# A decoder block on one core: seven products for the first ff2 block as well, and a new order around the output projection

## The chip, the cores and the metric

One core of a Trainium2 chip (trn2) runs one launch of the kernel. The metric is device time in microseconds (us), the median of 3 runs. Lower is better.

## What is computed

A post-norm decoder block on x of shape (1, 256, 2048), all in float32:

```
proj = x @ w_in                       # 2048 x 9216
q, k, v, u, vb, ga, gb = split(proj)
y_a = dilated_attention(q, k, v) @ w_proj_a
y_b = (u * spatial_gate(layer_norm(vb))) @ w_proj_b
mix = (sigmoid(ga) * y_a + sigmoid(gb) * y_b) @ w_out
h   = layer_norm(ALPHA * x + mix, ln1_gain, ln1_bias)
ff  = square(relu(h @ w_ff1 + b_ff1)) @ w_ff2 + b_ff2      # 2048 -> 8192 -> 2048
out = layer_norm(ALPHA * h + ff, ln2_gain, ln2_bias)
```

## The kernel before

**Chunks, pieces, steps.** Weights come from HBM in chunks of 512 rows by 512 columns (1 MB) through SP's DMA queue into three `raw` buffers. Float32 accuracy comes from a split: each number is a high part and a low part, and three matmuls (high by high, high by low, low by high) stand for one product. A chunk is two pieces of two k-tiles (128 rows each). For a piece ACT copies the high part (L188) and DVE subtracts to get the low part (`emit_low`, L157); both lie in one `w2` buffer. A step is one piece's matmuls. The lists `pieces` and `steps` are filled first; the main loop (L979 to 993) then writes, step by step: the splits for which a buffer is free (six ring buffers, so the splits run some five pieces ahead; a group can have spare buffers of its own as `tags`), the high and low parts of activations that wait in `rounds`, one or two finished tiles from `later`, the step's matmuls, and the side work that `at(step, ...)` put there. Each engine works off its own instructions in that order. A new chunk's load is issued when the last piece of a buffer is split.

**Groups.** A group is 512 output columns. With stationary weights (L252 with 512 columns, L254 with 256) run the in-projection, `w_pa`, `w_pb` and ff1; with stationary activations (L240 to 242) the output projection and ff2. When a weight-stationary group ends, ACT copies the half of each of its four banks (L273, with a bias L275), DVE adds (L277), and only then is a bank free.

**Seven products.** For the first two of four column groups, two row halves by two token halves by two column groups make eight block products; the kernel gets them by seven (P1 to P7) of 512 columns, as in Strassen's scheme (`products`, L634; L212 to 214 on PE). P1 uses the weight tile b0 as loaded, P5, P6 and P4 use it after one, two and three more blocks were added onto it, P7 uses b1, the sum of two blocks, and P3 and P2 use chunks. b0 and b1 are loaded and added to by POOL's DMA queue: `held_load` (L620; L623 loads, L625 accumulates onto b1) and `held_add` (L632, accumulates onto b0). The next block can be added onto b0 only when the low part of its last piece is made. The summed activations (`ca`) are made on DVE by `sum_of_acts` (L567, subtractions and additions at L575 to 578, high and low parts at L93 and L94). `collect` (L684) adds the products up at the very end for ff2, and behind P2 for the output projection.

**Order of the program.** In-projection with attention and gMLP between; then four times `w_pa` and `w_pb` (1024 rows, 8 pieces); the output projection's column group 2 in four chunks, with P7, P4, P3 and P2 behind one chunk each; its groups 0 and 1, then 3 (two passes, one for each token half); the first norm (`ln1_part`); ff1 of block 0 in two groups; then for b = 1 to 7 the two ff1 groups of block b and ff2 of block b-1 (1024 rows). Where block b-1 is in `SUMMED` (L608: blocks 1 to 6), its first two column groups are seven products, and `mixed(b)` (L696) lays the pieces of ff1 (F, 8 pieces for each group), of the products (2 each) and of ff2's columns 2 and 3 (E, 4 each) by the list ORDER (L37). I call such a stretch a period. Otherwise both ff1 groups come first, then four plain ff2 groups. P1, P6 and P5 of the output projection stand between `w_pa` and `w_pb`:

```
if i >= 2:
    add_product(("P1", "P6")[i - 2])      # behind w_pa's third and fourth group
...
if i == 2:
    at(len(steps), held_load, uo, 1)      # b1, behind w_pb's third group
    add_product("P5")
```

**The second residual.** The row tensors `y` hold the normalised rows. `residual2` makes for each of 4 column groups one bias part, b_ff2 += ALPHA * ln1_b, and for both token halves y = y * (ALPHA * ln1_g) and then y += that bias (L564, L565). The three vectors are broadcast over 128 partitions (1 MB each, the `wide` tiles) and loaded on SP's queue behind the ff1 chunks of block 1.

Of the kernel before, what the change touches and what calls it, by code (L numbers as in the profile page):

```python
# [26 lines left out]
G = 8  # L27
DB = G * 128
FF = 4 * D
CW = 512  # L30
# [5 lines left out]
NCT = CW // P  # L36
ORDER = ("F F F P1 F P1 F F F P5 F P5 F F F P6 F P6 F P3 P3 F P7 F P7 F "  # L37
         "E P2 E P2 E E P4 E P4 E E E").split()
WARM = (256, 256, 256, 128)
EARLY = 3  # L40
NBUCKET = 32
# [30 lines left out]
def block_kernel(ctx: ExitStack, tc: tile.TileContext, xT, x, w_in, rel_bias, lnv_g, lnv_b, wsT, b_sp,  # L72
# [61 lines left out]
    def add_group(g, sizes=None):  # L134
        hs = add_pieces(g, sizes)
        for h in hs:
            add_step(h, "all", h == hs[0], h == hs[-1])
# [162 lines left out]
    tiles = {}  # L300
# [252 lines left out]
    def load_wide(key, src, tag):  # L553
        tiles[key] = big.tile([P, D], F32, name="wide", tag=tag)
        nc.sync.dma_start(tiles[key], bcast(src, D))

    def residual2(c, part):
        sl = slice(c * CW, (c + 1) * CW)
        bb = tiles["b_ff2"][:, sl]
        if part == 0:  # L560
            nc.vector.scalar_tensor_tensor(bb, tiles["ln1_b"][:, sl], ALPHA, bb, op0=ALU.mult, op1=ALU.add)
        else:
            y = tiles["y", part - 1][:, sl]
            nc.vector.scalar_tensor_tensor(y, y, ALPHA, tiles["ln1_g"][:, sl], op0=ALU.mult, op1=ALU.mult)  # L564
            nc.vector.tensor_tensor(y, y, bb, op=ALU.add)  # L565

    def sum_of_acts(tags, ot, q):  # L567
# [37 lines left out]
        return ev  # L605

    NB = FF // 1024
    SUMMED = range(1, NB - 1)  # L608

    def ff_unit(blk):
        return SimpleNamespace(w=w_ff2, row=blk * 1024, act=lambda r, k: tiles["a", 2 * blk + r][:, k, :],
                               tags=("S10", "S11"), acc="S12", key="ff", scale=None)
# [81 lines left out]
    def mixed(b):  # L696

        made = {"F": [ff1_group(2 * b), ff1_group(2 * b + 1)], "E": [ff2(b - 1, c) for c in (2, 3)]}
        prods = products(ff_unit(b - 1), ff_unit(b) if b in SUMMED else None)
        if b - 1 == SUMMED[0]:  # L700
            for i in range(2):
                at(len(steps) - 7, held_load, ff_unit(b - 1), i)
        left = {}

        queue = {"F": [], "E": []}
        for name in ORDER:
            if name in prods:
                if name not in left:
                    hs = prods[name]()
                    left[name] = [(h, h == hs[0], h == hs[-1]) for h in hs]  # L710
                q = left[name]
            else:
                q = queue[name]
                if not q:
                    g = made[name].pop(0)
                    for c in range(g.nk // KC):
                        q.append((g, c, None))
                if q[0][2] is None:
                    g, c, _ = q.pop(0)
                    hs = add_pieces(g, None, (c,))  # L720
                    q[:0] = [(h, c == 0 and h == hs[0], c == g.nk // KC - 1 and h == hs[-1]) for h in hs]
            h, f, l = q.pop(0)
            add_step(h, "all", f, l)
# [71 lines left out]
    def quad(key):  # L795
        return lambda k: tiles[key][k // 4][:, k % 4, :]
# [5 lines left out]
    def at(s, f, *a):  # L802
        side.setdefault(s, []).append((f, a))
# [35 lines left out]
    def add_product(name):  # L839
        hs = prods[name]()  # L840
        for h in hs:
            add_step(h, "all", h == hs[0], h == hs[-1])

    at(len(steps) + 8, held_load, uo, 0)
    for i in range(4):
        add_group(Group(w_pa, i * CW, 8, quad("attnT"), "ws", ev_ya(i)))
        if i >= 2:
            add_product(("P1", "P6")[i - 2])
        if i == 2:
            for k in range(4):  # L850
                at(len(steps) - 1 + k, lambda k=k: sum_of_acts(("S6", "W"), k, tiles["G", 1][:, 0, k, :]))
        add_group(Group(w_pb, i * CW, 8, quad("gmlpT"), "ws", ev_yb(i), after=start_residual if i == 3 else None))
        if i == 2:
            at(len(steps), held_load, uo, 1)
            add_product("P5")

    g = Group(w_out, 2 * CW, 16, quad("merged"), "as", ev_out(2))
    for c, name in enumerate(("P7", "P4", "P3", "P2")):
# [7 lines left out]
                        ev_out(i, False), row=1024))  # L866


    spare = ("A0", "A1", "A2", "A3", "S6")
    wide = tuple(f"S1{i}" for i in range(4))  # L870
    at(len(steps), free.extend, spare)
    g = Group(w_out, 3 * CW, 16, quad("merged"), "as", ev_out(3), tags=spare)
# [17 lines left out]
        return Group(w_ff1, f * CW, 16, quad("hT"), "ws", ev_ff1(f))  # L890

    def ff1(f):
        add_group(Group(w_ff1, f * CW, 16, quad("hT"), "ws", ev_ff1(f), tags=wide if f == 1 else ()))

    def ff2(blk, c):
        return Group(w_ff2, c * CW, 8, lambda k: tiles["a", 2 * blk + k // NCT][:, k % NCT, :], "as",
                     ev_ff2(blk, c), row=blk * 1024, tags=LATE if blk == NB - 1 else ())

    ff1(1)
    s = len(steps)  # L900
    for i in range(4):
        for j in range(3):
            at(s + 13 + 3 * i + j, residual2, i, j)
    for b in range(1, NB):
        j = len(chunks)
        if b - 1 in SUMMED:
            mixed(b)
            continue
        ff1(2 * b)
        ff1(2 * b + 1)  # L910
        if b == 1:
            for i, a in enumerate((("ln1_b", ln1_b, "S11"), ("b_ff2", b_ff2, "S10"), ("ln1_g", ln1_g, "S12"))):
                load_post[j + 2 * i] = [lambda a=a: load_wide(*a)]
        for c in range(4):
            add_group(ff2(b - 1, c))
    at(len(steps), free.extend, LATE[:4])
# [111 lines left out]
```

## Time and profile before

| | before |
|---|---|
| median of 3 runs | 1326.16 us (1325.57 to 1326.43) |
| profiled execution | 1326.2 us, its span 1324.5 us |
| mean granted clock of TensorE | 0.998 |
| PE busy | 1312.9 us, 99% |
| DVE busy | 939.0 us, 71% |
| ACT busy | 691.0 us, 52% |
| DMA | 288.83 MB, mean 218 GB/s |

The span runs from the first to the last record of the profiled execution; its own time has 1.7 us more around it. PE is TensorE's matmuls, PEld its weight loads (beside them), DVE is VectorE, ACT is ScalarE, POOL is GpSimd (here almost only an issuer of DMAs), SP the engine that issues the other DMAs. A busy share is an average over stages; what bounds a stage is read from its waits. PE is at `w_pa` and `w_pb` until 527.88, then at the output projection until about 607, from 746.23 to 833.90 on the period of b = 2, and each later period takes 86.92.

### The profile page before, as it was taken

What the parts mean: (1) busy time and instruction counts of PE and PEld (TensorE: products, weight loads), DVE (VectorE), ACT (ScalarE), POOL (GpSimd) and SP (SyncE); (2) the same over time, 40 slices, a digit from 0 to 9 for tenths busy, and PEclk for the clock granted to TensorE, in tenths of its full rate; (3) what the DMA queues carried; (4) which work ended last, traced back from release to release, by engine and by line L of the source; (5) the groups of instructions that cost most, each with busy time, mean ns of one, the idle gap of its engine ahead of it and who ended that gap; (6) DMA issues with size and microseconds to landing.
All of it is one profiled execution on the core that took longest, in us unless ns stands there. A gap on an engine that the chain in (4) does not pass through costs nothing. (4 is left out here: it accounts for less than half of the span.)

```text
span 1324.5 us, 17423 instructions
## 1 busy us (share of the span) xinstructions
PE 1312.9 (99%) x6832; PEld 1111.0 (84%) x6832; DVE 939.0 (71%) x1426; ACT 691.0 (52%) x938; POOL 51.7 (4%) x57
## 2 busy tenths in 40 slices
PE   9999999999999999999999999999999999999998
PEld 6888888888888888889888888888888888888886
DVE  6554678565545689788769768678677796786776
ACT  4444465454544556545545366455555564555641
POOL 0000000000000001000000100010000000100000
PEclk9999999999999999999999999999999999999999
DMA  9866545546555569772874988987887879978561
GB/s 321 289 195 206 176 137 182 191 160 222 191 191 190 187 169 291 244 230 71 283 255 148 284 219 289 248 242 247 217 280 229 237 242 251 252 224 236 178 254 64
DMA packets 140003, 288.83 MB, mean 218 GB/s; under 512 B 5256, under 2 KB 7824, under 8 KB 139024
## 3 DMA queue, kind: packets, MB, share of 16 engines
q1 hardware_dynamic: 120592, 240.26, 53.5%
q0 software_dynamic: 19184, 47.20, 16.8%
q8 instruction: 53, 0.87, 0.3%
q10 hardware_dynamic: 144, 0.26, 0.1%
q14 instruction: 30, 0.25, 0.1%
HBM read 285.59 MB, written 2.11 MB: 217 GB/s over the span
## 5 line engine op out<-in xcount | busy, mean ns | idle before, releaser
L157 DVE TENSOR_TENSOR w<-raw,w 128x1024 fp32r<-128x1024 f32 (+1 forms) x438 | 529.2, 1218 | 300.8 <-ACT w L188 299.7
L188 ACT ACTIVATE w<-raw 128x1024 fp32r<-128x1024 f32 (+1 forms) x438 | 456.7, 1053 | 411.8 <-PE mm L254 289.7
L252 PE MATMUL mm<-hT,w 128*128 128x512 f32 x960 | 339.4, 394 | 0.8 <-DVE sum L277 0.8
L252 PE MATMUL mm<-xs,w 128*128 128x512 f32 x896 | 315.7, 395 | 0.0
L254 PE MATMUL mm<-hT,w 128*128 128x256 f32 x1024 | 276.0, 279 | 0.0
L254 PE MATMUL mm<-xs,w 128*128 128x256 f32 x896 | 250.0, 279 | 0.0
L252 PEld LDWEIGHTS mm<-hT,w 128*128 128x128 f32 x960 | 180.0, 187 | 44.3 <-DVE sum L277 1.1
L252 PEld LDWEIGHTS mm<-xs,w 128*128 128x128 f32 x896 | 167.9, 187 | 39.5
L254 PEld LDWEIGHTS mm<-hT,w 128*128 128x128 f32 x1024 | 188.0, 188 | 2.7
L254 PEld LDWEIGHTS mm<-xs,w 128*128 128x128 f32 x896 | 168.0, 187 | 0.2
L242 PE MATMUL mm<-w,a 128*128 128x512 f32 (+1 forms) x328 | 128.1, 390 | 0.0
L241 PE MATMUL mm<-w,a 128*128 128x512 f32 (+1 forms) x328 | 128.0, 390 | 0.0
L240 PE MATMUL mm<-w,a 128*128 128x512 f32 (+1 forms) x328 | 127.8, 390 | 0.0
L157 DVE TENSOR_TENSOR w<-held,w 128x1024 fp32r<-128x1024 f32 x70 | 85.6, 1223 | 39.3 <-ACT w L188 38.9
L188 ACT ACTIVATE w<-held 128x1024 fp32r<-128x1024 f32 x70 | 73.9, 1058 | 64.7 <-PE mm L242 26.6
L240 PEld LDWEIGHTS mm<-w,a 128*128 128x128 f32 x328 | 61.8, 188 | 14.3
L242 PEld LDWEIGHTS mm<-w,a 128*128 128x128 f32 x328 | 61.7, 188 | 14.0
L241 PEld LDWEIGHTS mm<-w,a 128*128 128x128 f32 x328 | 61.8, 188 | 13.9
L240 PE MATMUL mm<-w,xs 128*128 128x512 f32 x120 | 49.4, 412 | 0.3 <-ACT w L188 0.3
L241 PE MATMUL mm<-w,xs 128*128 128x512 f32 x120 | 47.7, 397 | 1.3 <-DVE w L157 1.3
L277 DVE TENSOR_TENSOR sum<-mm,half 128x256 f32<-128x256 f32 x136 | 48.9, 418 | 0.0
L242 PE MATMUL mm<-w,xs 128*128 128x512 f32 x120 | 47.6, 397 | 0.0
(193 smaller groups left out, 1512.8 us busy)
## 6 DMA issues: line engine op xcount, KB each, us to landing
raw<-in_w_ff_dram SPq DMA_DIRECT2D x116, 1024.0 KB, 6.5
raw<-in_w_in_dram SPq DMA_DIRECT2D x68, 1024.0 KB, 5.1
held<-in_w_ff_dram POOLq DMA_DIRECT2D x36, 1024.0 KB, 8.5
raw<-in_w_out_dram SPq DMA_DIRECT2D x14, 1024.0 KB, 5.4
raw<-in_w_pa_dram SPq DMA_DIRECT2D x8, 1024.0 KB, 5.1
raw<-in_w_pb_dram SPq DMA_DIRECT2D x8, 1024.0 KB, 5.1
held<-in_w_out_dram POOLq DMA_DIRECT2D x6, 1024.0 KB, 8.5
raw<-in_w_in_dram SPq DMA_DIRECT2D x6, 512.0 KB, 7.2
```

The source lines that it names most:

```text
L157: nc.vector.tensor_tensor(h["lo"], sl, f32(h["hi"]), op=ALU.subtract)
L188: nc.scalar.activation(h["hi"], source(h), AF.Copy)
L240: nc.tensor.matmul(p, ah, hi[:, kk, cs], start=first and kk == 0, stop=False)
L241: nc.tensor.matmul(p, ah, lo[:, kk, cs], start=False, stop=False)
L242: nc.tensor.matmul(p, al, hi[:, kk, cs], start=False, stop=last and kk == n - 1)
L252: nc.tensor.matmul(p, hi[:, kk, ws_], av, start=st, stop=False)
L254: nc.tensor.matmul(p[:, :S], lo[:, kk, ws_], av[:, :S], start=False, stop=en)
L277: nc.vector.tensor_tensor(s, p[:, :S], t, op=ALU.add)
```

## The change

- **Block 0 has seven products too** (SUMMED from 0). Its period (b = 1) follows a list of its own, FIRST: the products keep their order but P7, which comes behind P2.
- **The rows of the second norm's residual come earlier.** ln1_b and ln1_g are loaded, on SP's queue, into the buffers A2 and A3 ahead of the output projection's last group, which loses these two as spare buffers for its splits; b_ff2 comes near the end of the first ff1 group into S11. The second ff1 group keeps two spare buffers of four.
- **`residual2` is cut in two kinds of parts.** The factors (1, 2) lie beside the second ff1 group; the bias parts (0) and the additions (3, 4) lie in the first period.
- **Output projection.** P5 comes behind `w_pa`'s fourth group and P6 behind `w_pb`'s fourth (before: P5 behind `w_pb`'s third, P6 behind `w_pa`'s fourth). Summed activations are made in every second step. The load of b1 is written three steps ahead of the end of `w_pb`'s fourth group.
- **Held tiles of block 0** are loaded at the second step of the second ff1 group (b0) and at the 14th step of the period (b1).

```diff
 NCT = CW // P
 ORDER = ("F F F P1 F P1 F F F P5 F P5 F F F P6 F P6 F P3 P3 F P7 F P7 F "
          "E P2 E P2 E E P4 E P4 E E E").split()
+FIRST = ("F F F P1 F P1 F F F P5 F P5 F F F P6 F P6 F P3 P3 F "
+         "E P2 E P2 E F P7 E P7 F E P4 E P4 E E").split()
 WARM = (256, 256, 256, 128)
 EARLY = 3
 NBUCKET = 32
...
         bb = tiles["b_ff2"][:, sl]
         if part == 0:
             nc.vector.scalar_tensor_tensor(bb, tiles["ln1_b"][:, sl], ALPHA, bb, op0=ALU.mult, op1=ALU.add)
-        else:
+        elif part < 3:
             y = tiles["y", part - 1][:, sl]
             nc.vector.scalar_tensor_tensor(y, y, ALPHA, tiles["ln1_g"][:, sl], op0=ALU.mult, op1=ALU.mult)
+        else:
+            y = tiles["y", part - 3][:, sl]
             nc.vector.tensor_tensor(y, y, bb, op=ALU.add)
 
     def sum_of_acts(tags, ot, q):
...
         return ev
 
     NB = FF // 1024
-    SUMMED = range(1, NB - 1)
+    SUMMED = range(0, NB - 1)
 
 
 
...
 
         made = {"F": [ff1_group(2 * b), ff1_group(2 * b + 1)], "E": [ff2(b - 1, c) for c in (2, 3)]}
         prods = products(ff_unit(b - 1), ff_unit(b) if b in SUMMED else None)
-        if b - 1 == SUMMED[0]:
-            for i in range(2):
-                at(len(steps) - 7, held_load, ff_unit(b - 1), i)
         left = {}
 
         queue = {"F": [], "E": []}
-        for name in ORDER:
+        for name in FIRST if b == 1 else ORDER:
             if name in prods:
                 if name not in left:
                     hs = prods[name]()
...
     for i in range(4):
         add_group(Group(w_pa, i * CW, 8, quad("attnT"), "ws", ev_ya(i)))
         if i >= 2:
-            add_product(("P1", "P6")[i - 2])
+            add_product(("P1", "P5")[i - 2])
         if i == 2:
             for k in range(4):
-                at(len(steps) - 1 + k, lambda k=k: sum_of_acts(("S6", "W"), k, tiles["G", 1][:, 0, k, :]))
+                at(len(steps) - 1 + 2 * k, lambda k=k: sum_of_acts(("S6", "W"), k, tiles["G", 1][:, 0, k, :]))
         add_group(Group(w_pb, i * CW, 8, quad("gmlpT"), "ws", ev_yb(i), after=start_residual if i == 3 else None))
-        if i == 2:
-            at(len(steps), held_load, uo, 1)
-            add_product("P5")
+        if i == 3:
+            at(len(steps) - 3, held_load, uo, 1)
+            add_product("P6")
 
     g = Group(w_out, 2 * CW, 16, quad("merged"), "as", ev_out(2))
     for c, name in enumerate(("P7", "P4", "P3", "P2")):
...
                         ev_out(i, False), row=1024))
 
 
-    spare = ("A0", "A1", "A2", "A3", "S6")
+    spare = ("A0", "A1", "S6")
+    for i, a in enumerate((("ln1_b", ln1_b, "A2"), ("ln1_g", ln1_g, "A3"))):
+        at(len(steps) - 6 + 3 * i, load_wide, *a)
     wide = tuple(f"S1{i}" for i in range(4))
     at(len(steps), free.extend, spare)
     g = Group(w_out, 3 * CW, 16, quad("merged"), "as", ev_out(3), tags=spare)
...
         return Group(w_ff1, f * CW, 16, quad("hT"), "ws", ev_ff1(f))
 
     def ff1(f):
-        add_group(Group(w_ff1, f * CW, 16, quad("hT"), "ws", ev_ff1(f), tags=wide if f == 1 else ()))
+        add_group(Group(w_ff1, f * CW, 16, quad("hT"), "ws", ev_ff1(f), tags=wide[2:] if f == 1 else ()))
 
     def ff2(blk, c):
         return Group(w_ff2, c * CW, 8, lambda k: tiles["a", 2 * blk + k // NCT][:, k % NCT, :], "as",
                      ev_ff2(blk, c), row=blk * 1024, tags=LATE if blk == NB - 1 else ())
 
+
+    s = len(steps)
+    at(s - 10, load_wide, "b_ff2", b_ff2, "S11")
+    at(s + 1, held_load, ff_unit(0), 0)
     ff1(1)
-    s = len(steps)
+    e = len(steps)
     for i in range(4):
-        for j in range(3):
-            at(s + 13 + 3 * i + j, residual2, i, j)
+        for j in (1, 2):
+            at(s + 4 * (j - 1) + i, residual2, i, j)
+        at(e + i, residual2, i, 0)
+        for j in (3, 4):
+            at(e + 1 + i + 4 * (j - 3), residual2, i, j)
+    at(e + 13, held_load, ff_unit(0), 1)
     for b in range(1, NB):
-        j = len(chunks)
         if b - 1 in SUMMED:
             mixed(b)
             continue
         ff1(2 * b)
         ff1(2 * b + 1)
-        if b == 1:
-            for i, a in enumerate((("ln1_b", ln1_b, "S11"), ("b_ff2", b_ff2, "S10"), ("ln1_g", ln1_g, "S12"))):
-                load_post[j + 2 * i] = [lambda a=a: load_wide(*a)]
         for c in range(4):
             add_group(ff2(b - 1, c))
     at(len(steps), free.extend, LATE[:4])
```

On POOL, around the output projection (held_3848 is b0; held_4339 before and held_4510 after are b1; y are the two loads of x's rows), before:

```order
L623 DMA held_3848<-in_w_out_dram 128x4x512
L632 DMA held_3848<-in_w_out_dram 128x4x512 x2
L623 DMA held_4339<-in_w_out_dram 128x4x512
L625 DMA held_4339<-in_w_out_dram 128x4x512
L632 DMA held_3848<-in_w_out_dram 128x4x512
L499 DMA y_4589<-in_x_dram 128x2048
```

and with the change:

```order
L627 DMA held_3848<-in_w_out_dram 128x4x512
L636 DMA held_3848<-in_w_out_dram 128x4x512 x3
L627 DMA held_4510<-in_w_out_dram 128x4x512
L629 DMA held_4510<-in_w_out_dram 128x4x512
L501 DMA y_4569<-in_x_dram 128x2048
```

The third addition onto b0 stood behind b1's load and accumulation; it now stands ahead of both.

On ACT, around the splits of b1 for P7 (L188 is L190 with the change, the high part of a piece; L273 is L275, the halves of `w_pb`'s fourth group; acc gets P1 or P5), before:

```order
L188 ACTIVATE w2_4489<-raw_4328 128x1024
L188 ACTIVATE w2_4515<-held_4339 128x1024
L188 ACTIVATE w2_4535<-held_4339 128x1024
L188 ACTIVATE w2_4554<-raw_4410 128x1024
L273 ACTIVATE half_4573<-mm_4495 128x256
L273 ACTIVATE half_4577<-mm_4500 128x256
L273 ACTIVATE half_4581<-mm_4505 128x256
L273 ACTIVATE half_4585<-mm_4510 128x256
L188 ACTIVATE w2_4594<-raw_4410 128x1024
```

and with the change:

```order
L190 ACTIVATE w2_4454<-held_3848 128x1024
L665 ACTIVATE acc_4184<-aux_4447 128x512
L190 ACTIVATE w2_4465<-held_3848 128x1024
L190 ACTIVATE w2_4490<-raw_4251 128x1024
L190 ACTIVATE w2_4513<-raw_4251 128x1024
L190 ACTIVATE w2_4534<-held_4510 128x1024
L275 ACTIVATE half_4553<-mm_4470 128x256
L275 ACTIVATE half_4557<-mm_4475 128x256
L275 ACTIVATE half_4561<-mm_4480 128x256
L275 ACTIVATE half_4565<-mm_4485 128x256
L190 ACTIVATE w2_4574<-held_4510 128x1024
```

Both splits of b1 stood ahead of the four halves; now the second stands behind them, and P6's two splits of b0 stand a little ahead of b1's.

On DVE, one round in the new first period, with the change (sq is a squared tile of ff1, cb and ca the summed activations; y and wide belong to the residual; w2 is a piece):

```order
L601 SCALAR_TENSOR_TENSOR sq_5777<-sum_5722 128x256
L579 TENSOR_TENSOR cb_5779<-q0_5487,sq_5777 128x128
L580 TENSOR_TENSOR cb_5779<-q0_5487 128x128
L581 TENSOR_TENSOR cb_5779<-cb_5779,q0_5487 128x128
L582 TENSOR_TENSOR cb_5779<-sq_5777,cb_5779 128x128
L569 TENSOR_TENSOR y_4569<-y_4569,wide_5461 128x512
L563 SCALAR_TENSOR_TENSOR wide_5461<-wide_4887,wide_5461 128x512
L159 TENSOR_TENSOR w2_5802<-raw_5530,w2_5802 128x1024
L96 TENSOR_TENSOR a_5737<-sq_5777,a_5737 128x256
L96 TENSOR_TENSOR ca_5740<-cb_5779,ca_5740 128x2x128
L96 TENSOR_TENSOR ca_5741<-cb_5779,ca_5741 128x2x128
```

In block 0 there were no cb and ca before; the additions of the residual (L569) and its bias parts (L563) stand between them now.

## Rows read from the trace of the kernel before

**Rows 1.** First part of the page: busy us, share of the span, instructions.

```profile
PE 1312.9 (99%) x6832; PEld 1111.0 (84%) x6832; DVE 939.0 (71%) x1426; ACT 691.0 (52%) x938; POOL 51.7 (4%) x57
```

**Rows 2.** Timeline of PE: start us, duration, engine, line, operation, tile, shapes, count.

```profile
701.25 0.40 PE L240 MATMUL mm<-w,a 128*128 128x512 f32 x1
...
746.23 0.40 PE L252 MATMUL mm<-hT,w 128*128 128x512 f32 x1
```

**Rows 3.** Timeline of PE at three waits (in brackets: idle us, releaser).

```profile
501.31 0.40 PE L213 MATMUL aux<-w,ca 128*128 128x512 f32 x1
502.23 0.50 PE L214 MATMUL aux<-w,ca 128*128 128x512 f32 x1 [0.53 <-DVE ca L94]
...
634.15 0.28 PE L254 MATMUL mm<-hT,w 128*128 128x256 f32 x1
635.24 0.51 PE L252 MATMUL mm<-hT,w 128*128 128x512 f32 x1 [0.81 <-DVE sum L277]
...
768.65 0.39 PE L212 MATMUL aux<-w,ca 128*128 128x512 f32 x1
769.51 0.50 PE L213 MATMUL aux<-w,ca 128*128 128x512 f32 x1 [0.48 <-DVE w L157]
```

**Rows 4.** Timeline of ACT: halves and splits, output projection and second ff1 group.

```profile
514.44 0.92 ACT L273 ACTIVATE half<-mm 128x256 f32<-128x256 f32 x3
...
516.50 2.00 ACT L188 ACTIVATE w<-raw 128x1024 fp32r<-128x1024 f32 x2
...
631.40 2.01 ACT L188 ACTIVATE w<-raw 128x1024 fp32r<-128x1024 f32 x2 [6.20 <-DMA raw<-in_w_ff_dram]
```

**Rows 5.** Timeline of PE: first matmuls of w_pa 4, P6, w_pb 4, out 2, P7.

```profile
502.57 0.40 PE L252 MATMUL mm<-attnT,w 128*128 128x512 f32 x1
...
513.77 0.40 PE L212 MATMUL aux<-w,ca 128*128 128x512 f32 x1
...
516.57 0.39 PE L252 MATMUL mm<-gmlpT,w 128*128 128x512 f32 x1
...
527.88 0.40 PE L240 MATMUL mm<-w,merged 128*128 128x512 f32 x1
...
533.50 0.40 PE L212 MATMUL aux<-w,ca 128*128 128x512 f32 x1
```

**Rows 6.** Timeline of DVE: low part of P5's second piece (tile b0).

```profile
508.51 1.22 DVE L157 TENSOR_TENSOR w<-held,w 128x1024 fp32r<-128x1024 f32 x1
```

**Rows 7.** Timeline of POOL: issue of b1's accumulation and of b0's third sum.

```profile
508.07 1.26 POOL L625 DMA_DIRECT2D held<-in_w_out_dram  x1 [6.29 <-DMA held<-in_w_out_dram]
510.02 1.27 POOL L632 DMA_DIRECT2D held<-in_w_out_dram  x1 [0.69 <-DVE w L157]
```

**Rows 8.** Held tiles: issue to landing; whole run, then the two issues of rows 7.

```profile
DMA to landing us min/median/max: 5.5/8.5/18.0
...
DMA to landing us min/median/max: 8.9/11.6/14.2
```

**Rows 9.** POOL's DMA queue: packets, MB, share; 505 to 506 (load), 516 to 517 (accumulation).

```profile
q0 software_dynamic: 94, 0.39, 100.9%
...
q0 software_dynamic: 102, 0.20, 111.6%
```

**Rows 10.** The chain that ended last: start us, us, what.

```profile
749.05 18.01 DMA held<-in_w_ff_dram
```

**Rows 11.** Timeline of DVE: third ff1 group's sums; two rounds' beginnings in the next period.

```profile
700.93 1.45 DVE L277 TENSOR_TENSOR sum<-mm,half 128x256 f32<-128x256 f32 x4
...
708.89 0.42 DVE L597 SCALAR_TENSOR_TENSOR sq<-sum 128x256 f32<-128x256 f32 x1
...
713.75 0.42 DVE L597 SCALAR_TENSOR_TENSOR sq<-sum 128x256 f32<-128x256 f32 x1
```

**Rows 12.** Stretches: us, busy of PE, PEld, DVE, ACT, POOL, granted clock, DMA share, GB/s.

```profile
1313.00:1316.00 3.00, 3.00 (x9) 1.27 (x8) 2.76 (x8) 1.06 (x4) 0.00 (x0) 1.00 0.00 0
1318.50:1324.50 6.00, 1.35 (x2) 0.30 (x2) 1.77 (x4) 0.60 (x1) 0.00 (x0) 0.57 0.49 175
```

## The prediction

> **What bounds the kernel now.** The page's first part comes first: PE is busy for 99% of the span [rows 1]. Less work on another engine can therefore hardly shorten the run; a change counts by the matmuls that it takes from PE, and by the waits of PE that it removes or makes. The timeline of PE, read from start to start, gives both. In a run of 512-column matmuls nothing but the array sets the pace: 192 of them stand between 701.25 and 746.23, so 44.98/192 = 0.234 us each [rows 2]. (The 0.39 or 0.40 of a row is a duration; neighbours overlap.) Where two starts lie further apart, PE waited. The stretch that the change touches has three such places [rows 3]: 0.92 - 0.23 = 0.69 us at 501.31 (P5 of the output projection, for the low part of a summed activation), 1.09 - 0.12 = 0.97 us at 634.15 (the second ff1 group, for a PSUM bank that DVE had not emptied), and 0.86 - 0.23 = 0.63 us at 768.65 (P5 of the first period of products, for its held tile). Together that is 2.29 us.
>
> **Work taken from PE.** Block 0's first two ff2 groups were 2 x 8 x 2 x 3 = 96 matmuls of 512 columns; seven products are 7 x 4 x 3 = 84. Twelve fewer at 0.234 is **-2.8 us**. The ff1 and the other ff2 matmuls are the same ones in another order.
>
> **The three waits.** The first goes: P5 now comes after w_pa's fourth group, 11.2 us later [rows 5], and the last summed activation is issued only three steps later. The second goes: ACT made the two halves that empty the banks behind splits that waited 6.2 us for their DMA [rows 4]; with two buffers fewer those splits are issued behind the halves. The third goes: block 0's first held tile is loaded some five steps before its split, and nothing stands ahead of it on POOL. **-2.3 us**, if nothing is late in their place.
>
> **What is late next: P7 of the output projection.** POOL works its transfers off in order. Before, tile b1 (loaded, then accumulated upon) was issued ahead of the third sum into b0; now it stands behind that sum, which waits for the low part of P6's second piece, itself later than before. The terms, in the profile's time:
>
> - Without its 0.69 us PE reaches P7 at 533.50 - 0.69 = 532.8 [rows 3, 5]. Going back from there, out 2's first chunk takes 5.62, P6 2.80 and w_pb's fourth group 11.31 [rows 5]: P5 ends at 513.1 and gives P6's second piece its buffer.
> - From there to the end of its low part: before, 502.57 to 508.51 + 1.22 = 7.2 us [rows 5, 6], with ACT and DVE behind by their sums and gate products; with empty queues it is one split and one subtraction, 1.0 + 1.2 = 2.2 [rows 4, 6]. One round of sums, four evacuations and two gate products still stand ahead of it on DVE, so I take 6.0: 519.1.
> - POOL starts 0.3 later (509.73 to 510.02) and the sum holds it for 1.3 [rows 6, 7]: b1's load is issued at 520.7.
> - A transfer lands after 5.5 us at least [rows 8]: 526.2. Behind an accumulating one it is later: of the two issued at 508.07 and 510.02 one landed after 8.9 us and the other after 14.2, thus 7.2 us after the first [rows 7, 8]. So the load would follow the sum, which lands at 519.4 + 8.9 = 528.3; a load moves 0.39 MB in a us when it has the queue, an accumulation 0.20 [rows 9], so its 1.05 MB end 2.7 later, at 531.0. I take 530, nearer to this end, since the pair did queue.
> - The accumulation takes 8.9, up to 14.2 [rows 8]: 538.9. From a landing to the matmul that needs the low part it was 749.05 + 18.01 = 767.06 to 769.51, 2.45 us [rows 3, 10]: 541.4. P7's second matmul could have started at 533.0, so PE waits **8.3 us**.
> - On ACT the split that waits stands ahead of the four halves of w_pb's fourth group, and the second piece's split behind them. Four halves took 514.44 to 516.50, 2.06 us [rows 4]; with 1.15 on DVE the second piece comes 3.2 us behind the first, whose six matmuls cover 1.4: **1.8 us** more.
>
> P7's sum is +10.1. Its least is 513.1 + 2.2 + 0.3 + 1.3 + 5.5 + 8.5 (the median landing [rows 8]) + 2.45 - 533.0 = 0.4, and 1.8 more: 2.2. Its most is 513.1 + 7.2 + 1.6 + 10.3 + 14.2 + 2.45 - 533.0 = 15.9, and 1.8: 17.7. The two loads of x, behind it on POOL, are wanted only by P3's evacuation, some 20 us after P7; I take no wait for them.
>
> The Trainium skill, page "DMA: Bandwidth & Descriptors", section "Anatomy of one DMA — SWDGE (gpsimd) path", fits 2.0 us plus the bytes over 436 GB/s; for one megabyte that is an estimate of 4.4 us, load and accumulation would land at 529.5, PE would not wait for P7, and the sum would be 1322. The trace disagrees: the median of these transfers is 8.5 us and the least 5.5 [rows 8].
>
> **Block 0.** Seven products bring DVE 14 splits for 8, 16 small sums and 8 low parts, beside the residual's 20 parts, which it had before in a later place. Let T be the end of the second ff1 group. Before, the third group's four sums ended at 702.38, 1.1 us after its end at 701.25 [rows 2, 11]. Here a part and a split later the first round starts, at T + 2.9. A round with two parts took 713.75 - 708.89 = 4.86 [rows 11], which is as long as a round with a bias part and a factor now; the first lacks one and takes 4.1. Four rounds end at T + 21.6, and with a part (0.65) and a split (1.15) P5's first piece is whole at T + 23.4. PE comes to P5 after seven ff1 steps of 2.8 and two product steps of 1.4, at T + 22.4; with 0.23 to the second matmul it waits **0.7 us**. P5's second piece, whole at T + 25.2, releases the sum that P6 needs: 25.2 + 0.3 + 8.9 + 2.45 = T + 36.9, and P6 is due at T + 37.1. I take **0.3** (a sum of 14.2 us would make it 5). Block 0's P7 has some 26 us from P6's second piece, where this chain takes 22 to 28: no wait taken, up to 3 in the range.
>
> The three loads of rows and bias (1 MB each) move on SP to the output projection and ff1(0). The splits have a lead of five pieces there, some 14 us, which hides a chunk that comes later by one such load; without it, each would cost up to 2.7 us. The two spare buffers that they take cut a lead of 10 pieces to 8 in the last output group, and every piece is still split before its step. I take nothing, and 0 to 2 in the range.
>
> **Sum.** The profiled execution took 1326.2 (span 1324.5 and 1.7 around it), which is the median of the runs. 1326.2 - 2.8 - 2.3 + 10.1 + 1.0 = **1332.2 us**.
>
> **The rivals.**
>
> - *b1 is there in time (faster, the other side).* All as above, but load and accumulation need 9.9 us or less together from 520.7 (533.0 - 2.45 = 530.6 decides). PE doesn't wait: 1326.2 - 5.1 + 1.0 = 1322.1. For it: single transfers of 5.5 us occur. Against it: the shortest load and a median accumulation already make 14.0. It needs a step that I read wrongly. This is also what the skill's fit would give. Chance 0.15.
> - *DVE and ACT keep up.* With the sums spread over eight steps, P6's second piece is whole near 516, and P7 costs 2.2 to 6.7: 1324.3 to 1328.8. For it: the spread itself; against it: that the same work is still issued before the piece. Chance 0.20.
> - *The loss is larger.* b1's load follows the sum, its accumulation takes long, and block 0's P6 and P7 are late in the same way: 1334 to 1343. PE's clock may add to it. Up to PE's stop near the end the granted clock is 1.00, the 2.4 GHz level; after it 0.57 on average, close to the 1.2 GHz level [rows 12]. P7's twelve matmuls at the lower level would be 2.8 us more. Chance 0.22.
>
> The Trainium skill, page "TensorE: Matmul & The Clock Gate", Part 1, says that idling halves the clock until PE has worked again for a while; by it the forecast would be 1335.0. The trace agrees in its last microseconds [rows 12], and no row shows it for a stop of 8 us amid matmuls.
>
> **How the numbers follow.** A difference below 0.2%, 2.65 us, can't be told from none here. The forecast's own case, P7 late by 6.8 to 12 us, has 0.43, and its time is 1332.2. Slower is this case and the larger loss, 0.65; same is the second rival, 0.20; faster the first, 0.15. The range 1323.5 to 1337.5 leaves out the first rival and the far end of the third. The slower cases alone have 1329 to 1339.
>
> **What would show it.** In the changed kernel: POOL issues the third sum into b0 near 519, and b1's load and accumulation after it; PE stands still before P7 from about 533 for 6 us or more, released by DVE behind a split that waited for the DMA; the gaps of 501, 634 and 768 are gone; a gap under 1 us stands at block 0's P5. Wrong would be: no gap before P7 (the time is then near 1322), gaps of several us in block 0 alone, or the gaps apart no 2.8 us gained from block 0's periods.

## The result, and the profile after

| | before | changed |
|---|---|---|
| median | 1325.98 us (1325.57 to 1326.43, 4 runs) | 1337.13 us (1336.50 to 1337.21, 4 runs) |
| ratio | | 1.0083, 95% interval 1.0066 to 1.0100 |
| span of the profiled execution | 1324.5 us | 1335.5 us |
| PE's starts from `w_pa` to the second ff1 group | 428.98 to 632.85: 203.87 | 428.87 to 644.86: 215.99 |
| from there to the period of b = 2 | to 746.23: 113.38 | to 757.71: 112.85 |

The change is slower by 11 us. The forecast was 1332.2, slower, by the mechanism that the traces show; the size was 5 us short, and 1337.13 lies only 0.4 us inside the upper end of the range, 1337.5. The first part of the page of the changed kernel answers to [rows 1]:

```profile
PE 1314.0 (98%) x6820; PEld 1109.5 (83%) x6820; DVE 950.7 (71%) x1459; ACT 698.9 (52%) x952; POOL 58.4 (4%) x63
```

Twelve matmuls are gone, and PE is busy 1.1 us longer all the same; the rest of the 11 us is idle. The timeline of PE (start us, duration) finds both in one place, P7 of the output projection. These rows answer to [rows 5]:

```profile
532.36 0.39 PE L244 MATMUL mm<-w,merged 128*128 128x512 f32 x1
542.18 0.80 PE L214 MATMUL aux<-w,ca 128*128 128x512 f32 x1 [9.43 <-ACT w L190]
543.44 0.80 PE L215 MATMUL aux<-w,ca 128*128 128x512 f32 x1 [0.47 <-DVE w L159]
544.03 0.63 PE L216 MATMUL aux<-w,ca 128*128 128x512 f32 x1
...
546.45 0.79 PE L215 MATMUL aux<-w,ca 128*128 128x512 f32 x1
...
548.27 0.39 PE L242 MATMUL mm<-w,merged 128*128 128x512 f32 x1
```

P7 was due at 532.36 + 0.23 = 532.60 and should have ended 2.81 later, at 535.41; it ended at 548.27. That is **12.9 us** in one product. Its second matmul, which needs the first low part, came 10.6 us late (543.44 against 532.83), and the rest took 4.83 instead of 2.57, 2.3 more. Nothing on the way back is busy with work: the timelines of POOL and ACT show one thing waiting for the next. They answer to [rows 7] and [rows 4]:

```profile
519.03 1.26 POOL L636 DMA_DIRECT2D held<-in_w_out_dram  x1 [14.87 <-DVE w L159]
519.78 1.29 POOL L627 DMA_DIRECT2D held<-in_w_out_dram  x1
532.57 1.27 POOL L629 DMA_DIRECT2D held<-in_w_out_dram  x1 [11.50 <-DMA raw<-in_w_out_dram]
```

```profile
541.07 1.06 ACT L190 ACTIVATE w<-held 128x1024 fp32r<-128x1024 f32 x1 [21.30 <-DMA held<-in_w_out_dram]
542.03 0.91 ACT L275 ACTIVATE half<-mm 128x256 f32<-128x256 f32 x3
543.81 0.38 ACT L275 ACTIVATE half<-mm 128x256 f32<-128x256 f32 x1 [0.87 <-DVE sum L279]
544.09 1.05 ACT L190 ACTIVATE w<-held 128x1024 fp32r<-128x1024 f32 x1
```

The third sum into b0 (L636) goes out at 519.03, b1's load (L627) right behind it, and b1's accumulation (L629) only 12.8 us after the load. (The profile names a chunk as what ended that wait; the accumulation needs the load of its own tile, which lands at the same time, so the name is not to be trusted there.) ACT then waits 21.3 us for the tile, and the second piece's split stands behind the four halves.

In block 0's period four waits are left, seen in PE's timeline; the three of [rows 3] are gone:

```profile
689.76 0.39 PE L214 MATMUL aux<-w,ca 128*128 128x512 f32 x1
690.38 0.50 PE L215 MATMUL aux<-w,ca 128*128 128x512 f32 x1 [0.22 <-DVE w L159]
...
697.13 0.28 PE L256 MATMUL mm<-hT,w 128*128 128x256 f32 x1
698.80 0.49 PE L254 MATMUL mm<-hT,w 128*128 128x512 f32 x1 [1.39 <-DVE sum L279]
...
722.73 0.40 PE L214 MATMUL aux<-w,a 128*128 128x512 f32 x1
723.44 0.50 PE L215 MATMUL aux<-w,a 128*128 128x512 f32 x1 [0.32 <-DVE w L159]
...
734.54 0.39 PE L214 MATMUL aux<-w,ca 128*128 128x512 f32 x1
735.37 0.50 PE L215 MATMUL aux<-w,ca 128*128 128x512 f32 x1 [0.44 <-DVE w L159]
```

From start to start, less the matmul's own 0.23 or 0.12, they are 0.39 (P5), 1.55 (block 1's second ff1 group, for the banks of its first), 0.48 (P2) and 0.60 us (P7): 3.0 together. The sum by the trace is -2.8 (twelve matmuls) - 2.3 (three waits) + 12.9 + 3.0 = 10.8, against 11.0 between the spans.

### The profile page after: what moved, and what is told of

Its sections match the earlier page's. It is cut to its first block, busy times and chain, and to the rows that moved or that the text cites. A ratio compares the mean times of both kernels' runs of the same rounds, so it can differ in the third digit from the quotient of the medians.

```text
span 1335.5 us, 17467 instructions
## 1 busy us (share of the span) xinstructions
PE 1314.0 (98%) x6820; PEld 1109.5 (83%) x6820; DVE 950.7 (71%) x1459; ACT 698.9 (52%) x952; POOL 58.4 (4%) x63
## 5 line engine op out<-in xcount | busy, mean ns | idle before, releaser
L159 DVE TENSOR_TENSOR w<-raw,w 128x1024 fp32r<-128x1024 f32 (+1 forms) x434 | 523.5, 1217 | 277.4 <-ACT w L190 276.1
L190 ACT ACTIVATE w<-raw 128x1024 fp32r<-128x1024 f32 (+1 forms) x434 | 452.1, 1053 | 383.5 <-PE mm L256 267.7
L159 DVE TENSOR_TENSOR w<-held,w 128x1024 fp32r<-128x1024 f32 x80 | 97.7, 1222 | 62.3 <-ACT w L190 62.0
L190 ACT ACTIVATE w<-held 128x1024 fp32r<-128x1024 f32 x80 | 83.8, 1056 | 85.7 <-PE mm L244 22.9
L244 PE MATMUL mm<-w,a 128*128 128x512 f32 (+1 forms) x296 | 115.4, 390 | 0.0
L243 PE MATMUL mm<-w,a 128*128 128x512 f32 (+1 forms) x296 | 115.3, 390 | 0.0
L242 PE MATMUL mm<-w,a 128*128 128x512 f32 (+1 forms) x296 | 115.1, 389 | 0.0
L242 PEld LDWEIGHTS mm<-w,a 128*128 128x128 f32 x296 | 55.7, 188 | 12.8
L244 PEld LDWEIGHTS mm<-w,a 128*128 128x128 f32 x296 | 55.7, 188 | 12.6
L243 PEld LDWEIGHTS mm<-w,a 128*128 128x128 f32 x296 | 55.7, 188 | 12.4
L214 PE MATMUL aux<-w,ca 128*128 128x512 f32 x128 | 51.5, 402 | 9.4 <-ACT w L190 9.4
L215 PE MATMUL aux<-w,ca 128*128 128x512 f32 x128 | 51.8, 405 | 1.2 <-DVE w L159 1.1
L216 PE MATMUL aux<-w,ca 128*128 128x512 f32 x128 | 51.2, 400 | 0.0
L242 PE MATMUL mm<-w,xs 128*128 128x512 f32 x120 | 49.5, 412 | 0.1
```

What stands on the lines that cost most here:

```text
L159: nc.vector.tensor_tensor(h["lo"], sl, f32(h["hi"]), op=ALU.subtract)
L190: nc.scalar.activation(h["hi"], source(h), AF.Copy)
L214: nc.tensor.matmul(p, ah, hi[:, kk], start=first and kk == 0, stop=False)
L215: nc.tensor.matmul(p, ah, lo[:, kk], start=False, stop=False)
L216: nc.tensor.matmul(p, al, hi[:, kk], start=False, stop=last and kk == n - 1)
L242: nc.tensor.matmul(p, ah, hi[:, kk, cs], start=first and kk == 0, stop=False)
```

## The experiments

Ratios are to the kernel before, with their 95% interval.

**Is it the order on POOL?** In `e1_b1_early` one number of the changed kernel is another:

```diff
-            at(len(steps) - 3, held_load, uo, 1)
+            at(len(steps) - 10, held_load, uo, 1)
```

> The changed kernel with one number altered: the load of b1 for P7 is written ten steps ahead of the end of w_pb's fourth group instead of three, so that on POOL the load and its accumulation stand ahead of the third sum into b0. Theory (the order on POOL): the load starts near 504, the accumulation near 510, landed by about 520; P7 waits for nothing, its 12.9 us go, and the time is 1337.1 - 12.9 = 1324.2. Rival (POOL's queue is simply too slow for four transfers here, wherever they stand): the third sum then comes late to P4, or P7 still waits; 3 us or more of the 12.9 stay: 1327 to 1334.

Measured: 1323.91 us, ratio 0.9984 (0.9975 to 0.9993). POOL's timeline now has load, accumulation, third sum in that order:

```profile
507.53 0.78 POOL L627 DMA_DIRECT2D held<-in_w_out_dram  x1 [3.38 <-DVE cb L582]
516.33 1.26 POOL L629 DMA_DIRECT2D held<-in_w_out_dram  x1 [8.02 <-DMA held<-in_w_out_dram]
519.02 1.29 POOL L636 DMA_DIRECT2D held<-in_w_out_dram  x1 [1.44 <-DVE w L159]
```

Load and accumulation come later than I expected (507.5 and 516.3, not 504 and 510), and it is early enough: P7's first two matmuls start at 532.59 and 532.82, without a wait. The third sum goes out at the same time as in the changed kernel (519.02 and 519.03), so putting two transfers ahead of it did not hold back its issue. It did land later, 15.5 us after its issue instead of 9.1, but still ahead of P4, which PE reaches near 541 and which waits for nothing in the trace. The order alone is worth 13.2 us.

**Does all of the loss lie in the output projection?** `e2_out_alone` gives the kernel before only those edits, `e3_old_out` takes only those out of the changed one:

```diff
-            add_product(("P1", "P6")[i - 2])
+            add_product(("P1", "P5")[i - 2])
...
-                at(len(steps) - 1 + k, lambda k=k: sum_of_acts(("S6", "W"), k, tiles["G", 1][:, 0, k, :]))
+                at(len(steps) - 1 + 2 * k, lambda k=k: sum_of_acts(("S6", "W"), k, tiles["G", 1][:, 0, k, :]))
...
-        if i == 2:
-            at(len(steps), held_load, uo, 1)
-            add_product("P5")
+        if i == 3:
+            at(len(steps) - 3, held_load, uo, 1)
+            add_product("P6")
```

(as in `e2_out_alone`; `e3_old_out` is the reverse)

> The kernel before with the edits of the output projection alone (P5 behind w_pa's fourth group, P6 and b1's load as in the change, sums in every second step). Theory (the whole loss lies there): 1326.0 - 0.7 (the wait at 501) + 12.9 = 1338.2, and the span from the first ff1 group on looks as in the kernel before, shifted. Rival (part of the 12.9 comes from the loads of the norm's rows or from block 0): P7's wait is shorter by some us, 1330 to 1336.

> The changed kernel with the output projection's products in their former order; block 0's seven products, the rows' loads and the residual's parts stay as in the change. Theory: 1337.1 - 12.9 + 0.7 = 1324.9, with block 0's waits (1.55, 0.60, 0.48 and 0.39 us) still there: only about 1 us is gained by all the rest of the change. Rival (block 0's lateness hangs on what came before it): those waits change by over 1 us and the time leaves 1324 to 1326.

Measured: 1337.32 us for the edits alone, ratio 1.0087 (1.0072 to 1.0102), and 1324.58 without them, 0.9988 (0.9978 to 0.9997). PE's timeline of `e2_out_alone` has the same stop as the changed kernel, with nothing of block 0 or of the rows' loads in it:

```profile
532.63 0.39 PE L242 MATMUL mm<-w,merged 128*128 128x512 f32 x1
541.90 0.80 PE L212 MATMUL aux<-w,ca 128*128 128x512 f32 x1 [8.88 <-ACT w L188]
```

So this part loses 11.2 us by itself, and everything else in the change gains 1.5 together. Block 0's waits stay nearly as they were in `e3_old_out` (0.38, 1.55, 0.37 and 0.59 us), so they do not hang on what came before, against the rival there.

**Load or accumulation?** `e9_load_early_sum_late` writes only the load early and leaves the accumulation behind the third sum:

```diff
-            at(len(steps) - 3, held_load, uo, 1)
+            at(len(steps) - 10, held_load, uo, 1)
+            at(len(steps) - 3, held_second, uo)
```

(held_load issues no accumulation there, held_second issues it)

> The changed kernel with b1's load of the output projection written ten steps ahead of the end of w_pb's fourth group (as in e1_b1_early), and only its accumulation left where the change has it, behind the third sum into b0. It parts the 12.9 us between the load and the accumulation. Theory (each accumulating transfer in front costs what the pair before showed): the accumulation is issued at 519.8 instead of 532.6 and, second of a pair, lands after some 14 us, at 534; P7's second matmul starts at 536.4 instead of 532.8, and the second piece adds some 2.2: about 5.8 of the 12.9 us stay, 1329.7. Rival (only the load behind the sum was slow, an accumulation behind it is not): it lands after 9 us, P7 waits for nothing, 1324.

Measured: 1331.26 us, 1.0035 (1.0021 to 1.0049), 7.4 above `e1_b1_early`. The accumulation, issued at 520.03 right behind the sum, holds ACT's split back until 535.59, and P7 starts 3.9 us late and takes 6.0 instead of 2.8:

```profile
535.59 1.06 ACT L190 ACTIVATE w<-held 128x1024 fp32r<-128x1024 f32 x1 [15.59 <-DMA held<-in_w_out_dram]
```

That is the pair of [rows 8] again (14.2 us to the landing there, 15.5 here). Of the 13 us, some 7 hang on the accumulation standing behind the sum, and 6 more on the load standing there too. (How much of the 15.5 us is due to the two loads of x's rows, which go out behind the accumulation at 520.78 and 524.86, and to SP's chunk, no run shows.)

**What is the clock's part of P7?** In the changed kernel PE's clock falls in the stop. The windows (stretch, us, busy us of PE, PEld, DVE, ACT, POOL, granted clock, DMA share, GB/s) of the changed kernel:

```profile
520.00:532.00 12.00, 12.00 (x59) 9.92 (x58) 1.68 (x3) 0.00 (x0) 1.07 (x2) 1.00 0.97 259
532.00:542.00 10.00, 0.75 (x4) 0.27 (x2) 0.00 (x0) 0.93 (x1) 2.38 (x3) 0.77 0.82 187
542.00:548.30 6.30, 5.57 (x13) 3.61 (x13) 5.65 (x10) 4.29 (x10) 0.00 (x0) 0.55 0.50 211
```

1.00 is the 2.4 GHz level; in P7 itself 0.55 was granted, near the 1.2 GHz level, and its matmuls start 0.43 us apart instead of 0.23 (544.03 is followed by 544.46). `e4_pe_kept_busy` and `e7_pe_busy_own_bank` fill the stop with 40 matmuls whose result nobody reads, the first into a bank of its own, the second into P7's bank. The main edit of the second (`g.junk` is 40 for P7 and 0 elsewhere):

```diff
             if first:
                 sums["p"] = psx.tile([P, CW], F32, name="aux")
+                if g.junk:
+                    m = tiles["merged"][2][:, 0, :]
+                    for _ in range(g.junk):
+                        nc.tensor.matmul(sums["p"], m[:, :P], m, start=True, stop=True)
```

> The changed kernel with 40 matmuls of 512 columns more, whose result nobody reads, ahead of P7: they fill the 9.6 us in which PE stands still. Theory A (P7's twelve matmuls are slow for the second piece's late low part, and the lower clock matters little): they take 5.5 to 5.6 us instead of 6.09, and the time falls by about 0.5 us. Theory B (the lower clock makes most of the 3.3 us above the 2.8 of an undisturbed P7): they take about 3 us and the time falls by about 3 us.

> The changed kernel with 40 unused matmuls of 512 columns ahead of P7 of the output projection, written into P7's own bank, which P7's first matmul starts anew (in e4_pe_kept_busy they took a bank of their own, and P7 waited for ACT to empty the other one). They fill the 9.6 us stop. Theory A (P7's 6.09 us are set by the late low parts of its two pieces): P7 takes 5.5 to 5.7 us and the time falls by about 0.5 us, to 1336.6. Theory B (the lower clock makes most of the 3.3 us above 2.8): P7 takes about 3 us and the time is about 1334.

`e4_pe_kept_busy` answers nothing: 1341.24 us in its single run, because the extra bank was the second of only two, and P7 then waited for ACT to empty P6's, which ACT could do only at 548.27, behind the splits that waited. `e7_pe_busy_own_bank` took 1337.07 us, one run, the time of the changed kernel. The same stretches:

```profile
532.00:542.00 10.00, 9.74 (x43) 7.70 (x41) 0.00 (x0) 0.00 (x0) 2.38 (x3) 1.00 0.82 191
542.00:548.30 6.30, 3.15 (x10) 1.88 (x11) 4.53 (x9) 4.15 (x7) 0.00 (x0) 1.00 0.47 200
```

and PE's timeline:

```profile
543.30 0.50 PE L218 MATMUL aux<-w,ca 128*128 128x512 f32 x1 [1.56 <-ACT w L190]
544.55 0.50 PE L219 MATMUL aux<-w,ca 128*128 128x512 f32 x1 [0.76 <-DVE w L159]
...
547.57 0.50 PE L219 MATMUL aux<-w,ca 128*128 128x512 f32 x1 [0.77 <-DVE w L159]
...
548.84 0.40 PE L246 MATMUL mm<-w,merged 128*128 128x512 f32 x1
549.50 0.50 PE L247 MATMUL mm<-w,merged 128*128 128x512 f32 x1 [0.26 <-DVE w L159]
```

The clock stays at 1.00, and P7 takes 548.84 - 543.30 = 5.54 us instead of 6.09, as theory A had it: the second piece's low part sets its end at either clock. The lower clock cost 0.55 us of P7's 12.9, and hardly that much of the run: with the clock up, the next group's second matmul waits 549.50 - 548.84 - 0.23 = 0.43 us for its low part (it waits for nothing in the changed kernel), so all but some 0.1 us comes back right behind P7. (The time itself can't show so little: P7 started 1.1 us later in this run than in the changed kernel's.)

**What did block 0's seven products bring?** `e8_no_first_products` is `e1_b1_early` with the plain ff2 of block 0:

```diff
-    SUMMED = range(0, NB - 1)
+    SUMMED = range(1, NB - 1)
```

(and the held loads ahead of the first products where the kernel before has them)

> The kernel with b1 early (e1_b1_early), with block 0's ff2 computed plainly again (SUMMED from 1), the rows' loads and the residual's parts as in the change. It has twelve matmuls more, 2.8 us; the waits of the first period (0.38, 1.55, 0.50) go, and the 0.63 at the held tile of the first products comes back. Theory: 1323.9 + 2.8 - 2.4 + 0.6 = 1324.9, so block 0's products gain only about 1 us. Rival (the waits of the first period come from the residual's additions, not from the products): the 1.55 stays without them, and the time is 1326.5.

Measured: 1323.71 us, 0.9985 (0.9975 to 0.9994), no different from `e1_b1_early`; neither the theory's 1 us nor the rival's 2.6. From the second ff1 group to the period of b = 2 both take the same: 744.15 - 631.98 = 112.17 us with seven products, 744.19 - 631.92 = 112.27 without. Without them no wait is left in that stretch, and the 0.63 at the held tile does not come back either: its loads go out at 681 and 688 there, in the kernel before at 736. So the twelve matmuls (2.8 us) were paid for with waits (0.38 + 1.55 + 0.50 = 2.43). What both kernels gain over the kernel before, some 2.2 us, is the three waits of [rows 3], not the products.

**Why is DVE late in block 0's period?** DVE's timeline of the changed kernel shows what stood ahead of the four sums that empty the banks (L279; L569 are the residual's additions):

```profile
693.72 0.68 DVE L569 TENSOR_TENSOR y<-y,wide 128x512 f32<-128x512 f32 x1
694.32 1.22 DVE L159 TENSOR_TENSOR w<-raw,w 128x1024 fp32r<-128x1024 f32 x1
695.46 0.68 DVE L569 TENSOR_TENSOR y<-y,wide 128x512 f32<-128x512 f32 x1
696.06 2.35 DVE L159 TENSOR_TENSOR w<-raw,w 128x1024 fp32r<-128x1024 f32 x2
698.33 1.44 DVE L279 TENSOR_TENSOR sum<-mm,half 128x256 f32<-128x256 f32 x4
```

There is no idle time in it: DVE is a full queue behind PE. `e5_adds_late` moves the additions to where DVE has room, which needs another buffer for b1; `e6_adds_late_b1_early` also loads b1 of block 0 earlier, and `e11_adds_in_idle` puts the additions at steps 15 to 18:

```diff
-                               tags=("S10", "S11"), acc="S12", key="ff", scale=None)
+                               tags=("S10", "S11" if blk else "A3"), acc="S12", key="ff", scale=None)
...
-            at(e + 1 + i + 4 * (j - 3), residual2, i, j)
+            at(e + 19 + i, residual2, i, j)
...
-    at(e + 13, held_load, ff_unit(0), 1)
+    at(e + 4, held_load, ff_unit(0), 1)
```

(the last edit is not in `e5_adds_late`; `e11_adds_in_idle` has e + 14 + i)

> The kernel with b1 early (e1_b1_early) and, further, the residual's eight additions moved from the second to ninth step of the first period to its 20th to 23rd; b1 of block 0 lies in A3 instead of S11, so that the bias row can stay in S11 that long. Theory (DVE was 5 us behind in the first period for these additions, and so emptied the banks of block 1's first ff1 group late): the wait of 1.55 us goes, P5's 0.38 stays (the bias parts still lie ahead of it) and P7's 0.5 stays: 1323.9 - 1.55 = 1322.4. Rival (DVE is full in that stretch by the splits alone): the wait stays over 1 us and the time at 1323.9.

> As e5_adds_late, with b1 of block 0 loaded at the fifth step of the period instead of the 14th, which A3 allows: on POOL the load and its accumulation then stand ahead of the second and third sum into b0. Theory (P7 of block 0 waits 0.5 us only because its load stands behind the third sum, as in the output projection): that wait goes too: 1321.9. Rival (the second sum, now behind b1's accumulation, is late for P6): a new wait of 1 us or more at P6, 1322.5 or above.

> As e6_adds_late_b1_early, with the residual's eight additions at the 15th to 18th step of the first period instead of the 20th to 23rd: on DVE they then stand ahead of the splits that wait for a chunk (DVE is idle for 4.5 us before 706.87), not between the splits behind them. Theory (the 0.64 us wait that e6_adds_late_b1_early still has at 717 comes from the additions between those splits): it goes, from the second ff1 group to the third period it takes 109.6 us, and the time is 0.6 us below 1322.4, near 1321.8; the spread of a single run (about 1 us, from the first transfers of the program) can hide that in the median, not in the trace. Rival (the chunk itself is late there): the wait stays.

Measured: 1322.06, 1322.45 and 1322.81 us; ratios 0.9973 (0.9963 to 0.9983), 0.9975 (0.9966 to 0.9985) and 0.9974 (0.9964 to 0.9984). The bank wait is gone in all three, so the additions made it. P5's 0.38 and P7's 0.5 are gone too in `e5_adds_late`, where I had expected both to stay; a new wait makes up for them, so that its time came out near the forecast by luck. P7's load still stands behind the third sum there, so `e6_adds_late_b1_early` can't show what P7's wait came from. What took the place of these waits, in PE's timelines of `e5_adds_late`, `e6_adds_late_b1_early` and `e11_adds_in_idle`:

```profile
716.06 0.39 PE L254 MATMUL mm<-hT,w 128*128 128x512 f32 x1
717.79 0.39 PE L256 MATMUL mm<-hT,w 128*128 128x256 f32 x1 [1.34 <-DVE w L159]
```

```profile
717.36 0.39 PE L254 MATMUL mm<-hT,w 128*128 128x512 f32 x1
718.23 0.39 PE L256 MATMUL mm<-hT,w 128*128 128x256 f32 x1 [0.48 <-DVE w L159]
```

```profile
690.65 0.39 PE L214 MATMUL aux<-w,ca 128*128 128x512 f32 x1
691.31 0.50 PE L215 MATMUL aux<-w,ca 128*128 128x512 f32 x1 [0.28 <-DVE w L159]
...
700.99 0.39 PE L214 MATMUL aux<-w,ca 128*128 128x512 f32 x1
702.08 0.50 PE L215 MATMUL aux<-w,ca 128*128 128x512 f32 x1 [0.70 <-DVE w L159]
```

The stretch from the second ff1 group to the period of b = 2 takes 111.02, 110.18 and 111.56 us (112.17 in `e1_b1_early`, 112.27 without the products; without any wait it would be 113.38 - 0.97 - 2.81 = 109.6). `e6_adds_late_b1_early` is the best there, and its second sum, behind b1's accumulation, is not late. My reason for the rest was wrong: with the additions out of the way in `e11_adds_in_idle`, 0.52 us of the wait near 717 stays, and P6 and P3 wait instead. What makes the wait near 717 stays open; in `e5_adds_late` ACT's splits stood idle for 7.17 us until 705.34, for a chunk, but no run parts the chunk from the rest. The medians can't rank the three, for the first transfers of the program differ from run to run: `w_pa` starts at 428.81 in the trace of `e5_adds_late` and at 430.09 in that of `e6_adds_late_b1_early`. All three beat both kernels, by 0.27% at best over the kernel before and by 15 us over the changed one.

**Is the list FIRST needed?** `e10_usual_order` is `e1_b1_early` without it:

```diff
-        for name in FIRST if b == 1 else ORDER:
+        for name in ORDER:
```

> The kernel with b1 early (e1_b1_early), and block 0's period by the common list ORDER instead of FIRST, so that P7 comes ahead of P2. There P7 is due some 16 us earlier, near 705. Theory (b1 of block 0 has no time to spare: its load, behind the third sum, ends near 706 and its accumulation near 718): PE waits about 13 us for P7, 1337. Rival (FIRST is not needed): no more than 1 us, 1325.

Measured: 1336.09 us, 1.0071 (1.0048 to 1.0094). That is 12.2 us above `e1_b1_early`. PE stops for P7 of block 0 as it did for that of the output projection, for 9.83 us in front of it. What ends the stop is the emptying of a product's bank (L665), which on ACT stands behind b1's first split, and that starts at 715.12, when the tile has landed. With the slow matmuls behind it is 12.9 us in this trace (16.22 us from 706.77 to 722.99, where 3.28 were due):

```profile
706.77 0.28 PE L256 MATMUL mm<-hT,w 128*128 128x256 f32 x1
716.72 0.79 PE L214 MATMUL aux<-w,ca 128*128 128x512 f32 x1 [9.67 <-ACT acc L665]
717.49 0.80 PE L215 MATMUL aux<-w,ca 128*128 128x512 f32 x1
...
722.99 0.39 PE L254 MATMUL mm<-hT,w 128*128 128x512 f32 x1
```

## Why the prediction was right, and where it was short

- **The twelve matmuls and the three waits** (-2.8 and -2.3): as forecast. Each of the three is gone from the trace.
- **The place and mechanism of the loss**: as forecast. The third sum went out at 519.03 (forecast 519.4), b1's load at 519.78 (520.7), and PE stopped before P7, due at 532.60 (532.8).
- **The step that was too small is the load's landing.** "I take 530, nearer to this end" had 9.3 us for a load behind the sum, and 531.0 as its upper end. It landed after 12.5 us, at 532.3, and the accumulation went out after 12.8. The landing of the sum itself was right (9.1 us; 8.9 taken). What failed is the rate after it: 0.39 MB in a us [rows 9] holds when the load has the DMA engines for itself. The DMA queues of the changed kernel (packets, MB, share of 16 engines) while the sum moved, until 528.1:

```profile
q0 software_dynamic: 585, 1.28, 83.1%
q1 hardware_dynamic: 176, 0.33, 11.3%
```

  and from 528.1 to 532.3, when it had landed:

```profile
q0 software_dynamic: 215, 0.82, 49.2%
q1 hardware_dynamic: 382, 0.76, 48.2%
```

  SP's chunk, held up meanwhile, took half the engines, and the load ran at 0.82 / 4.2 = 0.20 MB in a us. At 0.39 the same 0.82 MB would have landed at 528.1 + 2.1 = 530.2 by my estimate, which is the forecast's 530. A chunk that also wants the engines was missing from my step. (The shares are read from the trace; no run takes the chunk away.)
- **The accumulation and the rest of the chain** (8.9 and 2.45): 532.57 to 541.07 is 8.5, and 2.37 from there to the second matmul. So the wait was 10.6 instead of 8.3.
- **The second piece** (1.8): 2.3 in the changed kernel, of which the clock is 0.55; 1.7 at full clock in `e7_pe_busy_own_bank` (548.84 - 544.55 - 2.57). P7's term is 12.9 instead of 10.1.
- **The clock.** Third rival: "P7's twelve matmuls at the lower level would be 2.8 us more." They did run near that level and it cost 0.55 at most, for the price was added to a wait that covers it. The rule that I weighed there (the Trainium skill, page "TensorE: Matmul & The Clock Gate", Part 1) agrees with this trace in what it says of idling: 0.77 was granted in the stop and 0.55 behind it. Its addition to the sum was mine, and too much.
- **Block 0** (+1.0 forecast, +3.0 measured). P5's 0.7 was 0.39, P6's 0.3 nothing. The step that failed is that I followed DVE's queue only to the products: the sums that empty the banks of block 1's ff1 group stand in the same queue, and they made the 1.55. P7's 0.60 lies within the 3 that I kept for the range. P2's 0.48 I had not seen.
- **The rivals.** That b1 is in time: ruled out by the rows above. By the fit of the Trainium skill, page "DMA: Bandwidth & Descriptors", section "Anatomy of one DMA — SWDGE (gpsimd) path", the transfers would have needed 4.4 us each, by an estimate; load and accumulation landed after 12.5 and 8.4 us here. The likeliest case had P7 late by 6.8 to 12 us; with 12.9 and block 0's 3.0 the time came out in the lower half of the "larger loss", 1334 to 1343, a case with a chance of 0.22. So the direction and the mechanism were forecast; that the size still fell inside the range, by 0.4 us, was luck.

## What to carry to other kernels

A queue that is worked off in order makes the tile that is wanted soon wait for whatever the one ahead of it waits for: before moving work in the list, ask of each queue which of its transfers is now behind one that depends on that work, and price a transfer behind another with the other queue's loads as well. One number, ten steps instead of three, was the difference between 1337 and 1324 us here. And when work is added to an engine that is already a full queue, look for every one of its consumers, not only those of the new work: the PSUM banks of the next group were the ones to wait.

## What was not expected of the hardware

- What was issued 0.75 us behind an accumulating transfer of POOL's queue landed some 7 us later than it did with none in front. In the changed kernel the load there landed after 12.5 us, where the load issued at 610.47 with nothing in front landed after 5.6; in `e9_load_early_sum_late` the accumulation there landed after 15.5 us, where that of the changed kernel landed after 8.4. Other queues moved data in each of these stretches, so the difference is not the accumulation's alone.
- Whether a lower clock costs anything is decided by what PE waits for behind the stop. In the changed kernel it was 0.55 us at most, as the low parts were late anyway. In `e10_usual_order` only the low part for P7's second matmul was late behind the stop of 9.83 us (the matmul starts at 717.49, 0.54 us late); of the 12.9 us some 2.6 are the slow matmuls'. Its window of that stretch:

```profile
716.70:723.00 6.30, 6.28 (x17) 4.67 (x18) 6.09 (x7) 5.64 (x6) 0.79 (x1) 0.50 0.30 90
```

  PE is busy all through it at the 1.2 GHz level.
